# Seven block products for the first 1024 rows of the first layer's output projection

## The chip, the cores and the metric

The kernel runs on one core of a Trainium2 chip. The metric is the device time of one execution in microseconds (us). Before the change three runs gave 829.10, 829.45 and 830.46 us, a median of 829.45 us.

## The reference, cut to what matters

Four residual layers on an input of 256 positions by 1024 channels, all in float32. Layers 0 and 3 are the gated MLP below, layer 1 is an attention layer, layer 2 a pooling layer.

```python
def mixer_a(h, w_in, v_gain, w_s, b_s, w_out):
    proj = h @ w_in                                   # (256, 1024) @ (1024, 6144)
    u, v, z = proj[..., :2048], rms_norm(proj[..., 2048:4096], v_gain), proj[..., 4096:]
    ...                                               # mixed: lower-triangular ws over 128 positions, plus b_s
    y = u * mixed * jax.nn.silu(z)
    return y @ w_out                                  # (256, 2048) @ (2048, 1024)

def reference(x, norm_gain, a_w_in, ...):
    for i in range(4):
        h = rms_norm(x, norm_gain[i])
        y = mixer(i)(h, ...)                          # A, B, C, A
        x = x + y
    return x
```

The change concerns `y @ w_out` of layer 0, and of that the first 1024 of the 2048 rows of `w_out`.

## The kernel before

**One product.** TensorE (PE) multiplies in a rounded 32-bit format. Each float32 operand is kept as a high part (rounded) and a low part (the rest), and one product is three matmuls: high by high (L87), high by low (L88), low by high (L89), in `mm3`. A matmul has 128 rows of the contraction, 128 positions and at most 512 columns.

**The weight stream.** All weights come in one sequence of units of 512 KB (128 partitions, two contraction blocks, 512 columns). SyncE (SP) issues a load into one of four raw buffers (`wr`; `load_units`, L177), ScalarE (ACT) writes the high part `w..h` (L92), VectorE (DVE) the low part `w..l` (L95). Seven pairs of high and low parts exist. A raw buffer is free for the next load when the low part of its unit is done, so the load of unit i follows the low part of unit i − 4. In layer 3 two more raw buffers take part. Units are split up to five ahead of the matmuls that use them.

**The order of work.** Each engine does its instructions in the order in which the program writes them. The program writes in steps: each step emits the matmuls of half a unit, lets the tasks that are due emit theirs (`tick`), and then emits splits for coming units. A task that gives a number waits for so many ticks. So a DVE instruction emitted by a task stands behind all splits that were emitted before it.

**Accumulators.** Four PSUM banks (`pp`, one 128x512 float32 result each) take the projections, three take attention and mixing, and one takes transposes (`yp`). A bank is given to the next user when the reader of its last content is done.

**Layer 0.** Units 0 to 15 are v, 16 to 47 alternate z and u in four groups of 512 columns, 48 to 63 are `w_out` ("wo"), 64 is the first of layer 1. Group n of y is made by `y_task`: two DVE multiplications by u (L664), four by the mixed values (L669, shown as pairs), four transposes on PE for each half of the positions (`yp`, L677), a high part on ACT and a low part on DVE (`y0nh`, `y0nl`). Group 3, the last, is made while wo already runs. `proj_out` takes 16 contraction blocks against two column halves: a unit holds two blocks and one column half and is used for both halves of the positions, 12 matmuls of 128x512. Four accumulators `wo` stay open through it; the last four blocks are done position half by position half, and DVE adds each accumulator into the residual `x` (L546).

**Block products that exist already.** In layer 3 three of the z/u groups are done as seven products of half-sized blocks in place of eight (`seven_products`). They need sums of the quarters of the weights, which `sums_of_quarters` makes long before: it loads a quarter of a part's columns into a buffer (`stage`, or `qs`, which shares the buffer `xs`), makes four additions on DVE (L194), and stores the sums to DRAM (`sums`); `PARTS` says how many such parts are made beside layers 0, 1 and 2. They also need sums of quarters of h (12 DVE passes of 128x512 with four high parts on ACT).

Of the kernel before, what the change touches and what calls it, by code (L numbers as in the profile page):

```python
# [17 lines left out]
P = 128  # L18
# [28 lines left out]
SEVEN = (0, 2, 3)  # L47
PARTS = (4, 8, 8)
# [3 lines left out]
def hybrid_trunk_kernel(ctx, tc, x, wts, norm_gainT, a_v_gain, a_wsT, a_bsT, b_gl, b_gv, c_scaleT,  # L52
# [92 lines left out]
    sums = {(n, j): dp.tile([4, P, UNIT], F32, name=f"sums{n}{j}") for n in SEVEN for j in range(2)}  # L145

    def seven_units(n):

        return n_units - 48 + 8 * n + (8 if n == 3 else 0)

    for n in reversed(SEVEN):
        z = seven_units(n)
        seq[z:z + 8] = [e[j] for e in (((n, 0, 0), (n, 0, 1)), (z, z + 1), (z + 6, z + 7), ((n, 3, 0), (n, 3, 1)),
                                       (z + 2, z + 3), ((n, 2, 0), (n, 2, 1)), ((n, 1, 0), (n, 1, 1)))
                        for j in range(2)]
    n_seq = len(seq)

    raw_users = {"wr": [-1] * RAW_BUFS, "xs": [-1], "wx": [-1]}

    def raw_place(i):  # L160

        return ("wr", "wr", "wr", "wr", "xs", "wx")[i % 6] if i >= n_units - 48 else "wr"
# [18 lines left out]
    def sums_of_quarters(parts, shared=False, delay=0, wait=2):  # L181
# [5 lines left out]
        for n, j, c in parts:  # L187
            z = seven_units(n) + j
            cs = slice(c * 256, (c + 1) * 256)
            q = cp.tile([P, 4, 256], F32, tag="xs", name=f"qs{n}{j}{c}", bufs=1) if shared else stage  # L190
            nc.sync.dma_start(q, wts[z:z + 8:2][:, :, cs].rearrange("i p c -> p i c"))
            yield 7
            for a, b in ((0, 2), (2, 3), (3, 0), (1, 3)):
                nc.vector.tensor_tensor(q[:, a], q[:, a], q[:, b], op=ALU.add)  # L194
                yield 1
            yield wait
            nc.sync.dma_start(sums[n, j][:, :, cs].rearrange("i p c -> p i c"), q)
            yield 4
# [318 lines left out]
    def proj_out(layer, nkt, yT, k0=0):  # L517


        acc = [[[(slice(0, HALF), pp(f"wo{layer}_{t}{n}"))] for n in range(2)] for t in range(2)]  # L520
# [4 lines left out]
        for j in range(k0 // 2, jt):  # L525
            for n in range(2):
                w = next_unit()
                for kk in range(2):
                    k = 2 * j + kk
                    for t in range(2):  # L530
                        for cs, o in acc[t][n]:
# [6 lines left out]
        for t in range(2):  # L538
            for i, (j, n, w) in enumerate(tail):
# [26 lines left out]
                tick()  # L566

# [15 lines left out]
    def layer_a(layer, consts, pl, mid):  # L583
# [101 lines left out]

        if layer == DEPTH - 1:
            smh, sml = pair(pl, [P, 4, 4, P], "sm", f"sm{layer}", 1)

        def sums_task():
            q = {}  # L690
            for k, t in ((1, 1), (0, 1), (0, 0), (1, 0)):
                d = q[k, t] = tmp("sz", f"sq{layer}{k}{t}", 4).rearrange("p (k c) -> p k c", c=P)
# [669 lines left out]
```

## Time and profile before

| | |
|---|---|
| median of three runs | 829.45 us |
| the profiled execution's own time | 829.75 us |
| its span | 828.0 us |
| PE busy | 821.5 us |
| DVE busy | 612.7 us |
| ACT busy | 515.0 us |
| first matmul of wo in layer 0 | 147.67 us |
| first matmul of layer 1 (`qk`) | 193.05 us |

The span is the time from the first to the last instruction that the profiler saw; 1.75 us of the profiled execution lie around it. In a timeline row the first number is the start in microseconds, the second the time that the row took, then come the engine, the line, the operation, output <- inputs by the program's names, the shape, and how many instructions the row joins; in square brackets, how long the engine had been idle and who released it. The start of a matmul counted from the start of the one before is what PE needs for one; the durations of neighbours overlap. The same holds for DVE, where a row's duration is a little longer than the distance to the next.

### The profile page before, as it was taken

How to read it: one execution, taken by the hardware profiler on the slowest of the kernel's cores; microseconds unless marked ns; L12 is line 12 of the kernel's file. 1: busy time of each engine (PE TensorE's matmuls, PEld its weight loads, DVE VectorE, ACT ScalarE, POOL GpSimd, SP SyncE). 2: the span in 40 equal slices, each digit the busy share in tenths (PEclk: the TensorE clock that was granted, in tenths of full speed). 3: DMA queues.
4: the chain of work that ended last, by engine and by line, in shares of the span. 5: the costliest groups of instructions: out<-in, count | busy, mean ns of one | idle time of the engine just before them, and what ended most of it. 6: DMA issues, size and time to landing. Idle time of an engine off the chain costs nothing.

```text
span 828.0 us, 12649 instructions
## 1 busy us (share of the span) xinstructions
PE 821.5 (99%) x4585; PEld 711.2 (86%) x4585; DVE 612.7 (74%) x1054; ACT 515.0 (62%) x947; POOL 46.3 (6%) x69
## 2 busy tenths in 40 slices
PE   9999999999999999999999999999999999999998
PEld 7888888888988888888888889999988888788887
DVE  5887656646768678678678577798874799979683
ACT  7775444436768687687688567436643668656570
POOL 1201000000000010010010012000000000000000
PEclk9999999999999999999999999999999999999999
DMA  8878666662888668577567268647786378868661
GB/s 280 289 270 274 225 224 192 219 200 79 296 269 255 200 201 275 184 225 257 190 199 222 78 200 286 224 159 236 227 284 220 102 249 276 284 206 323 204 261 51
DMA packets 70111, 184.21 MB, mean 222 GB/s; under 512 B 5952, under 2 KB 31312, under 8 KB 69920
## 3 DMA queue, kind: packets, MB, share of 16 engines
q1 hardware_dynamic: 68784, 179.33, 65.1%
q0 software_dynamic: 976, 3.79, 1.4%
q8 instruction: 36, 0.59, 0.3%
q10 hardware_dynamic: 288, 0.28, 0.2%
q14 instruction: 27, 0.22, 0.1%
HBM read 169.74 MB, written 13.63 MB: 221 GB/s over the span
## 4 chain that ended last, share of the span: by engine, by line
PE 98%; DMA 1%; DVE 0%; issue 0%; POOL 0%; ACT 0%; ACTq 0%
PE qk L89 5%; PE qk L87 5%; PE qk L88 5%; PE wo L87 5%; PE wo L88 5%; PE wo L89 5%; PE v L88 5%; PE v L87 5%; PE v L89 5%; PE z L89 2%; PE z L87 2%; PE u L87 2%; PE u L88 2%; PE z L88 2%; PE u L89 2%; PE cz L89 2%
## 5 line engine op out<-in xcount | busy, mean ns | idle before, releaser
L849 POOL TENSOR_TENSOR qr<-qm,m 128x8 f32<-128x8 f32 x12 | 20.1, 1674 | 228.1 <-DVE qm L848 228.1
L844 ACT ACTIVATE junk<-qk 128x128 bf16<-128x128 f32 x96 | 26.6, 277 | 5.6 <-PE qk L89 3.0
L853 ACT ACTIVATE qn<-qk,qr 128x128 f32<-128x128 f32 x96 | 27.5, 381 | 3.7 <-POOL qr L849 3.7
L194 DVE TENSOR_TENSOR stage<-stage 128x256 f32<-128x256 f32 x64 | 26.9, 421 | 2.6 <-DMA stage<-in_wts_dram 2.1
L320 ACT ACTIVATE hT<-hp,gT 128x128 fp32r<-128x128 f32 x48 | 13.0, 384 | 14.9 <-PE hp L316 14.9
L546 DVE TENSOR_TENSOR x<-wo,x 128x512 f32<-128x512 f32 (+1 forms) x16 | 10.8, 674 | 13.3 <-PE wo L89 13.3
L302 POOL TENSOR_TENSOR r<-ms,m 128x1 f32<-128x1 f32 x6 | 4.2, 708 | 273.9 <-DVE ms L299 273.9
L325 DVE SCALAR_TENSOR_TENSOR hT<-hp,gT,hT 128x128 fp32r<-128x128 f32 x48 | 13.5, 344 | 7.4 <-ACT hT L320 7.4
L844 ACT ACTIVATION_READ_ACCUMULATOR junk<-qk 128x1 f32 x96 | 18.9, 197 | 0.0
L294 ACT ACTIVATE junk<-x 128x512 bf16<-128x512 f32 x16 | 10.2, 639 | 10.1 <-DVE x L546 9.9
L194 DVE TENSOR_TENSOR qs<-qs 128x256 f32<-128x256 f32 x32 | 13.4, 419 | 3.6 <-DMA qs<-in_wts_dram 3.5
L848 DVE TENSOR_SCALAR qm<-qs 128x8 f32<-128x8 f32 x12 | 2.1, 172 | 18.4 <-ACT junk L844 18.4
L943 ACT ACTIVATE p<-p,rl 128x384 f32<-128x384 f32 (+1 forms) x16 | 11.5, 769 | 6.1 <-DVE rl L942 6.1
L664 DVE SCALAR_TENSOR_TENSOR sz<-u,m,sz 128x512 f32<-128x512 f32 x8 | 6.0, 746 | 11.7 <-PE u L89 11.7
L874 PE MATMUL qt<-ident,qn 128*128 128x128 f32 x96 | 14.5, 274 | 0.1
L874 PEld LDWEIGHTS qt<-ident,qn 128*128 128x128 f32 x96 | 11.3, 140 | 3.2 <-issue 1.4
L866 DVE TENSOR_TENSOR rb<-qn,kcb 128x32 f32<-128x32 f32 x96 | 13.8, 186 | 0.0
L602 DVE TENSOR_TENSOR vv<-v,kc 128x512 f32<-128x512 f32 x16 | 10.7, 686 | 3.4 <-ACT junk L600 3.1
L939 ACT ACTIVATE p<-p,nb 128x768 f32<-128x768 f32 x8 | 7.5, 938 | 7.3 <-DVE nb L938 7.3
L862 DVE TENSOR_TENSOR ra<-qn,kcb 128x64 f32<-128x64 f32 x48 | 10.6, 221 | 0.8 <-ACT qn L853 0.2
L974 PE MATMUL pt<-ident,p 128*128 128x128 f32 x48 | 9.9, 275 | 0.0
L797 ACT ACTIVATE sz<-z,m 128x512 f32<-128x512 f32 x8 | 5.4, 688 | 6.9 <-PE z L89 6.9
(2963 smaller groups left out, 3349.1 us busy)
## 6 DMA issues: line engine op xcount, KB each, us to landing
wr<-in_wts_dram SPq DMA_DIRECT2D x258, 512.0 KB, 4.4
wr<-sums SPq DMA_DIRECT2D x20, 512.0 KB, 4.6
stage<-in_wts_dram SPq DMA_DIRECT2D x16, 512.0 KB, 5.1
sums<-stage SPq DMA_DIRECT2D x16, 512.0 KB, 6.2
qs<-in_wts_dram SPq DMA_DIRECT2D x8, 512.0 KB, 5.3
sums<-qs SPq DMA_DIRECT2D x8, 512.0 KB, 5.0
wx<-in_wts_dram SPq DMA_DIRECT2D x7, 512.0 KB, 5.4
wx<-sums SPq DMA_DIRECT2D x4, 512.0 KB, 4.5
```

The lines of the kernel that those rows point to most:

```text
L87: nc.tensor.matmul(out_ap, lh[0], rh[0], start=start, stop=False, skip_group_check=True)
L88: nc.tensor.matmul(out_ap, lh[0], rh[1], start=False, stop=False, skip_group_check=True)
L89: nc.tensor.matmul(out_ap, lh[1], rh[0], start=False, stop=stop, skip_group_check=True)
L194: nc.vector.tensor_tensor(q[:, a], q[:, a], q[:, b], op=ALU.add)
L320: nc.scalar.activation(h_parts(layer)[0][:, k, t * P:(t + 1) * P], pt[:, k % 4], AF.Copy, scale=gT[:, layer, k:k + 1])
L325: nc.vector.scalar_tensor_tensor(hTl, pt[:, k % 4], gT[:, layer, k:k + 1], hTh.bitcast(F32), op0=ALU.mult, op1=ALU.subtract)
L844: nc.scalar.activation(junk[:, :HD], ov[t][:, h], AF.Square, accum_out=ssq[t][:, h:h + 1])
L849: nc.gpsimd.tensor_tensor(rqs, ms, m05_row[:, :8], op=ALU.pow)
L853: nc.scalar.activation(qn[t][:, h], ov[t][:, h], AF.Copy, scale=rq[t][:, h:h + 1])
L866: nc.vector.tensor_tensor(rb[:, hs, s0:s0 + 16], qn[t][:, hs, s1:s1 + 16], c, op=ALU.mult)
L874: nc.tensor.transpose(pts[t][:, h], qn[t][:, h], ident)
L943: nc.scalar.activation(f, f, AF.Copy, scale=rl[i][:, 0:1])
```

## The change

The first 1024 rows of `w_out` (units 48 to 55 before: eight units of 12 matmuls of 128x512, 96 in all) are taken as a two by two block product of four blocks of y (position half by 512 rows) with four blocks of weights (512 rows by 512 columns), and done as seven products of 12 matmuls, 84 in all. Each product takes two units, and a unit is used for 6 matmuls. Eight of the fourteen units hold sums of the weight quarters and are loaded from DRAM (`sums`); the stream has 14 units there in place of 8. The other half of `w_out` follows as before, 8 units (62 to 69), and layer 1 begins with unit 70.

- The products go into four banks: `xw` (used for three products, the second and third being added on the first), `yw`, `zw` (two) and `ww`. After each product DVE adds or subtracts the bank's content into `x`, eight additions in all. `proj_out` takes its four banks when it first uses them.
- Sums of blocks of y are made by `y_sums` from `left_sums`, as in layer 3: 12 DVE passes and four high parts on ACT, while z and u of the last groups run. It uses `wx` and one new tile.
- Sums of weight quarters: beside layer 0 there were 4 parts, now there are 12, in two chains that begin after the first v projection; one works in `stage` on 8 parts, the other in `xs` on 4. `PARTS` goes from (4, 8, 8) to (8, 4, 8, 8). A part is 0.5 MB in, four additions, 0.5 MB out. The longer chain runs on through wo.
- `sums_task` of layer 3 becomes a call of the common `left_sums`; its order of work stays.

```diff
-SEVEN = (0, 2, 3)
-PARTS = (4, 8, 8)
+BLOCKS = {("wo", 0): 48, ("zu", 0): -48, ("zu", 2): -32, ("zu", 3): -16}
+PARTS = (8, 4, 8, 8)
...
-        acc = [[[(slice(0, HALF), pp(f"wo{layer}_{t}{n}"))] for n in range(2)] for t in range(2)]
+        acc = [[[], []], [[], []]]
+
+        def bank(t, n):
+            if not acc[t][n]:
+                acc[t][n].append((slice(0, HALF), pp(f"wo{layer}_{t}{n}")))
...
+    def part_product(o, a, first):
+        for j in range(2):
+            w = next_unit()
+            for kk in range(2):
+                k = 2 * j + kk
+                mm3(o, a(k), (w[0][:, kk], w[1][:, kk]), first and k == 0, k == 3)
+                step(kk, due=kk == 1)
...
+    def proj_seven(layer, yT, smh, sml):
+        def add(t, n, o, op=ALU.add):
+            xh = xt[t][:, n * HALF:(n + 1) * HALF]
+            nc.vector.tensor_tensor(xh, xh, o, op=op)
+            yield 1
+
+        def quarter(k, t):
+            return lambda i: yT(4 * k + i, t)
+
+        xb = pp(f"xw{layer}")
+        part_product(xb, quarter(0, 0), True)
+        spawn(add(0, 0, xb), 1)
+        yb = pp(f"yw{layer}")
+        part_product(yb, quarter(1, 0), True)
+        spawn(add(0, 0, yb), 1)
+        need(("sums", layer))
+        zb = pp(f"zw{layer}")
+        part_product(zb, sum_tile(smh, sml, S_A21_A22), True)
+        spawn(add(1, 1, zb), 1)
+        part_product(xb, sum_tile(smh, sml, S_REST), False)
+        spawn(add(0, 1, xb, ALU.subtract), 1)
+        part_product(zb, sum_tile(smh, sml, S_A12_REST), False)
+        spawn(add(0, 1, zb), 1)
+        part_product(xb, sum_tile(smh, sml, S_A11_A21), False)
+        spawn(add(1, 1, xb, ALU.subtract), 1)
+        spawn(add(1, 0, xb), 1)
+        wb = pp(f"ww{layer}")
+        part_product(wb, quarter(1, 1), True)
+        spawn(add(1, 0, wb), 1)
...
+            if layer == 0 and n == 0:
+                spawn(sums_of_quarters(parts[:4] + parts[8:8 + PARTS[1]], False, 8, 1, 6))
+                spawn(sums_of_quarters(parts[4:8], True, 15, 1, 6))
...
-        if layer == 0:
-            spawn(sums_of_quarters(parts[:PARTS[0]]))
+        def y_sums():
+            while ("y", layer, 1) not in done:
+                yield 1
+            room = [wx[:, 0], wx[:, 1], tmp("yq", "yq", 1)]
...
+            yield from left_sums(layer, y_quarter, place, smh, sml, ("sums", layer), 2)
+
         for n in range(4):
+            if n == 2 and ("wo", layer) in BLOCKS:
+                spawn(y_sums(), 4)
...
-        proj_out(layer, 16, get, KT if layer == DEPTH - 1 else 0)
+        if ("wo", layer) in BLOCKS:
+            proj_seven(layer, get, smh, sml)
+        proj_out(layer, 16, get, KT if layer == DEPTH - 1 or ("wo", layer) in BLOCKS else 0)
```

What this makes of the order on DVE, around the start of wo. Before, the rows from the last group's multiplications on (`sz` and `yy` are the two multiplications, `w53l` the low part of unit 53, `y03l` the low part of y's last group, one row for each half of the positions):

```order
L664 SCALAR_TENSOR_TENSOR sz_1264<-u_0_1268,m_77,sz_1264 128x512
L669 SCALAR_TENSOR_TENSOR yy_1363<-mx_1306,bs_267,sz_1264 128x256 x2
L664 SCALAR_TENSOR_TENSOR sz_1266<-u_1_1269,m_77,sz_1266 128x512
L669 SCALAR_TENSOR_TENSOR yy_1367<-mx_1313,bs_267,sz_1266 128x256 x2
L95 TENSOR_TENSOR w53l<-wr_1287,w53h 128x1024
L95 TENSOR_TENSOR y03l<-yp_1390,y03h 128x4x128
L95 TENSOR_TENSOR w54l<-wr_1321,w54h 128x1024
L95 TENSOR_TENSOR y03l<-yp_1415,y03h 128x4x128
L95 TENSOR_TENSOR w55l<-wr_1340,w55h 128x1024
L95 TENSOR_TENSOR w56l<-wr_1359,w56h 128x1024
L95 TENSOR_TENSOR w57l<-wr_1397,w57h 128x1024
```

After it only low parts of units stood there. Now, behind the same four rows of multiplications (in the changed file L97 is the low part, L198 the addition of weight quarters, L636 the addition into x):

```order
L198 TENSOR_TENSOR stage<-stage 128x256
L97 TENSOR_TENSOR w53l<-wr_1345,w53h 128x1024
L198 TENSOR_TENSOR stage<-stage 128x256
L97 TENSOR_TENSOR w54l<-wr_1379,w54h 128x1024
L198 TENSOR_TENSOR stage<-stage 128x256
L97 TENSOR_TENSOR y03l<-yp_1451,y03h 128x4x128
L636 TENSOR_TENSOR x<-x,xw_1427 128x512
L97 TENSOR_TENSOR w55l<-wr_1397,w55h 128x1024
L198 TENSOR_TENSOR stage<-stage 128x256
L97 TENSOR_TENSOR w56l<-wr_1415,w56h 128x1024
L97 TENSOR_TENSOR y03l<-yp_1486,y03h 128x4x128
L636 TENSOR_TENSOR x<-x,yw_1460 128x512
```

Four additions of quarters and the first additions into x have come in between, and `y03l` has moved from behind one low part to behind two. Further on DVE, rows that follow at once:

```order
L97 TENSOR_TENSOR w57l<-wr_1439,w57h 128x1024
L97 TENSOR_TENSOR w58l<-wr_1458,w58h 128x1024
L636 TENSOR_TENSOR x<-x,zw_1495 128x512
L97 TENSOR_TENSOR w59l<-wr_1474,w59h 128x1024
L97 TENSOR_TENSOR w60l<-wr_1493,w60h 128x1024
L636 TENSOR_TENSOR x<-x,xw_1427 128x512
L97 TENSOR_TENSOR w61l<-wr_1508,w61h 128x1024
L97 TENSOR_TENSOR w62l<-wr_1521,w62h 128x1024
L636 TENSOR_TENSOR x<-x,zw_1495 128x512
L97 TENSOR_TENSOR w63l<-wr_1534,w63h 128x1024
L97 TENSOR_TENSOR w64l<-wr_1546,w64h 128x1024
L636 TENSOR_TENSOR x<-x,xw_1427 128x512 x2
```

Two low parts stand ahead of each addition; behind these rows come `w65l`, `w66l` and the addition of `ww`. On PE, at the second unit of the second half of `w_out` (`wo_00` to `wo_11` are its four accumulators, by position half and column half; L89, L90 and L91 are the three matmuls of a product in the changed file):

```order
L91 MATMUL wo_10_1630<-w62h,y02l 128x512
L89 MATMUL wo_01_1648<-w63h,y02h 128x512 [waits DVE_49,Activation_49]
L90 MATMUL wo_01_1648<-w63l,y02h 128x512
L91 MATMUL wo_01_1648<-w63h,y02l 128x512
L89 MATMUL wo_11_1652<-w63h,y02h 128x512 [waits DVE_49]
```

The first matmul of `wo_01` and of `wo_11` waits for the addition that empties the bank it takes over, those of `xw` and `ww`; one unit earlier `wo_10` waits in the same way for that of `zw`. Before, the four accumulators of wo were open from its start, and nothing in wo waited for an addition. On SP, the same stretch of the changed program's queue (`sums` are the stored sums):

```order
L181 DMA wr_1493<-sumswo_69 128x1024
L181 DMA wr_1508<-sumswo_70 128x1024
L201 DMA sumszu_71<-stage 128x4x256
L181 DMA wr_1521<-in_wts_dram 128x1024
L181 DMA wr_1534<-in_wts_dram 128x1024
L181 DMA wr_1546<-in_wts_dram 128x1024
L181 DMA wr_1559<-in_wts_dram 128x1024
L195 DMA stage<-in_wts_dram 128x4x256
L181 DMA wr_1572<-in_wts_dram 128x1024
```

A store of 0.5 MB of sums now goes ahead of the load of unit 62 (`wr_1521`), and a load of a part ahead of that of unit 66 (`wr_1572`). Before, no transfer of the chain stood in this stretch of the queue.

More of the change, by code (lines that the diff above doesn't have):

```diff
@@ L517, in proj_out @@
     def proj_out(layer, nkt, yT, k0=0):
-        acc = [[[(slice(0, HALF), pp(f"wo{layer}_{t}{n}"))] for n in range(2)] for t in range(2)]
+        acc = [[[], []], [[], []]]
+        def bank(t, n):
+            if not acc[t][n]:
+                acc[t][n].append((slice(0, HALF), pp(f"wo{layer}_{t}{n}")))
+        if ("wo", layer) not in BLOCKS:
+            for t in range(2):
+                for n in range(2):
+                    bank(t, n)
         if layer == DEPTH - 1:
@@ L566, in proj_out, with left_sums, full, parted @@
                 tick()
+    S_A21_A22, S_A11_A21, S_REST, S_A12_REST = range(4)
+    def left_sums(name, quarter, place, smh, sml, key, pause=1):
+        def full(k, t):
+            d = place(f"sq{name}{k}{t}").rearrange("p (k c) -> p k c", c=P)
+            hh, hl = (a.bitcast(F32) for a in quarter(k, t))
+            nc.vector.tensor_tensor(d, hh, hl, op=ALU.add)
+            return d
+        def parted(i, d):
+            hi_of(smh[:, i], d)
+            yield pause
+            lo_of(sml[:, i], d, smh[:, i])
+            yield pause
+        a22 = full(1, 1)
+        yield pause
+        a21 = full(0, 1)
+        yield pause
+        nc.vector.tensor_tensor(a22, a21, a22, op=ALU.subtract)
+        yield from parted(S_A21_A22, a22)
+        a11 = full(0, 0)
+        yield pause
+        nc.vector.tensor_tensor(a21, a11, a21, op=ALU.subtract)
+        yield from parted(S_A11_A21, a21)
+        nc.vector.tensor_tensor(a11, a22, a11, op=ALU.subtract)
+        yield from parted(S_REST, a11)
+        a12 = full(1, 0)
+        yield pause
+        nc.vector.tensor_tensor(a12, a12, a11, op=ALU.add)
+        yield from parted(S_A12_REST, a12)
+        done.add(key)
@@ L712, in sm @@
             def sm(i):
-                return lambda k: (smh[:, i, k], sml[:, i, k])
-            def product(o, a, first):
-                for j in range(2):
-                    w = next_unit()
-                    for kk in range(2):
-                        k = 2 * j + kk
-                        mm3(o, a(k), (w[0][:, kk], w[1][:, kk]), first and k == 0, k == 3)
-                        step(kk, due=kk == 1)
+                return sum_tile(smh, sml, i)
+            product = part_product
             def minus(o, name):
@@ L1045, in layer_b @@
                 if hp == 0 and g == 0:
-                    n1, n2 = sum(PARTS[:2]), sum(PARTS)
-                    spawn(sums_of_quarters(parts[PARTS[0]:n1]))
+                    n0, n1, n2 = (sum(PARTS[:i]) for i in (2, 3, 4))
+                    spawn(sums_of_quarters(parts[n0:n1]))
                     spawn(sums_of_quarters(parts[n1:n2], True, 9))
@@ L1205, in hybrid_trunk_kernel @@
     box = {}
-    parts = [(n, j, c) for n in SEVEN for j in range(2) for c in range(4)]
+    parts = [(b, j, c) for b in BLOCKS for j in range(2) for c in range(4)]
     def after_ws():
```

71 lines of the change are left out of this document (34 added, 37 removed).

## The prediction

> **What bounds the kernel now.** I read the busy shares, the granted clock and the chain that ended last, then PE's waits, then the windows of the stretches that the change touches, then the timelines there.
>
> ```profile
> PE 821.5 (99%) x4585; PEld 711.2 (86%) x4585; DVE 612.7 (74%) x1054; ACT 515.0 (62%) x947; POOL 46.3 (6%) x69
> PEclk9999999999999999999999999999999999999999
> PE 98%; DMA 1%; DVE 0%; issue 0%; POOL 0%; ACT 0%; ACTq 0%
> PE warm L286 <- DVE wx L65: 1.1, 1, 1.1
> PE xb L87 <- ACT n L725: 0.7, 1, 0.7
> ```
>
> PE is busy 821.5 of 828.0 us at full clock and makes 98% of the last chain. Its longest wait inside the layers is 0.7 us, in layer 3's seven products. So a matmul taken away is worth its time, if PE meets no new wait.
>
> ```profile
> 47.00:147.00 100.00, 100.00 (x477) 83.68 (x476) 67.55 (x90) 49.70 (x58) 4.25 (x8) 1.00 0.71 233
> 147.00:176.00 29.00, 29.00 (x133) 24.03 (x132) 17.76 (x19) 11.47 (x12) 0.00 (x0) 1.00 0.62 206
> 697.00:717.00 20.00, 19.35 (x91) 15.90 (x91) 19.84 (x21) 15.23 (x19) 1.44 (x2) 1.00 0.88 309
> ```
>
> The columns are length, PE, weight loads, DVE, ACT, POOL, clock, DMA share, GB/s. DVE, at 74% overall, is busy 17.76 of 29 us where wo begins (147 to 176), and 19.84 of 20 in a seven-product stretch of layer 3 (697 to 717). The question is what happens when the first becomes like the second.
>
> **What is saved.** A unit of wo:
>
> ```profile
> 147.67 0.39 PE L87 MATMUL wo<-w48h,y00h 128*128 128x512 f32 x1
> 159.52 0.39 PE L87 MATMUL wo<-w52h,y01h 128*128 128x512 f32 x1
> 162.24 0.39 PE L87 MATMUL wo<-w53h,y01h 128*128 128x512 f32 x1
> ```
>
> Unit 52 to 53 is 2.72 us for 12 matmuls, 0.2267 each. 96 become 84: **−2.72 us**. From 48 to 52 there are 11.85 us, four units and two sets of transposes, so a set costs (11.85 − 10.88)/2 = 0.485.
>
> The Trainium skill ("TensorE: Matmul & The Clock Gate", section "Wait — 56ns, not 53.3ns?") gives 215.7 ns from one matmul of 512 columns to the next; by that the saving would be 2.59 us. The trace's 226.7 ns does not agree, and decides.
>
> **What it adds to DVE before wo.** By the order, 20 more additions of quarters, plus 12 passes for the sums of y, fall before the last group's multiplications. Prices:
>
> ```profile
> 63.16 0.88 DVE L194 TENSOR_TENSOR stage<-stage 128x256 f32<-128x256 f32 x2
> 63.95 1.22 DVE L95 TENSOR_TENSOR w24l<-wr,w24h 128x1024 fp32r<-128x1024 f32 x1
> 65.09 0.88 DVE L194 TENSOR_TENSOR stage<-stage 128x256 f32<-128x256 f32 x2
> 708.28 0.69 DVE L753 TENSOR_TENSOR p<-yb,p 128x512 f32<-128x512 f32 x1
> 708.88 1.22 DVE L95 TENSOR_TENSOR w239l<-wx,w239h 128x1024 fp32r<-128x1024 f32 x1
> ```
>
> From start to start an addition of quarters takes 0.79/2 = 0.395, a low part 1.14, a pass of 128x512 0.60. That is 20 x 0.395 + 12 x 0.60 = 15.1 us in the 100 us from 47 to 147, where DVE is busy 67.55. It fits, also with twice the transfers:
>
> ```profile
> 198.00:248.00 50.00, 50.00 (x321) 45.13 (x320) 34.80 (x74) 35.48 (x84) 3.40 (x2) 1.00 0.77 253
> 73.42 1.23 DVE L95 TENSOR_TENSOR w28l<-wr,w28h 128x1024 fp32r<-128x1024 f32 x1 [3.83 <-ACT w28h L92]
> 86.96 0.39 PE L87 MATMUL u<-w28h,hT 128*128 128x512 f32 x1
> ```
>
> From 198 to 248 two such chains run and PE loses nothing. Unit 28, the one whose split came latest for its load, was ready at 74.65 and first used at 86.96: 12.3 us of cover. I cost this part at nothing; if loads came more than 12 us late it would cost the excess.
>
> **What it adds to DVE in the seven products.** A unit now lasts 6 x 0.2267 = 1.36 us on PE; its low part takes 1.14 on DVE, so little is left for eight additions into x, four of quarters and two low parts of y. Ahead of them stand the last multiplications of y:
>
> ```profile
> 147.19 0.75 DVE L664 SCALAR_TENSOR_TENSOR sz<-u,m,sz 128x512 f32<-128x512 f32 x1 [3.91 <-PE u L89]
> 147.98 0.88 DVE L669 SCALAR_TENSOR_TENSOR yy<-mx,bs,sz 128x256 f32<-128x256 f32 x2
> 148.77 0.74 DVE L664 SCALAR_TENSOR_TENSOR sz<-u,m,sz 128x512 f32<-128x512 f32 x1
> 149.55 0.88 DVE L669 SCALAR_TENSOR_TENSOR yy<-mx,bs,sz 128x256 f32<-128x256 f32 x2
> 150.34 1.22 DVE L95 TENSOR_TENSOR w53l<-wr,w53h 128x1024 fp32r<-128x1024 f32 x1
> ```
>
> They wait for u (3.91 us idle), so DVE enters at 147.19 as before and comes out at 150.34.
>
> ```profile
> 154.88 0.69 DVE L95 TENSOR_TENSOR y03l<-yp,y03h 128x512 fp32r<-128x512 f32 x1 [1.04 <-ACT y03h L92]
> ```
>
> A `y03l` takes 0.69 until what waits for it may start, and 0.60 until the next row, like the other passes of 128x512. From 150.34 I add up the new order at the prices above, in the clock of before; PE starts the first product at 147.67, and each product takes 2.72.
>
> 1. *Transposes.* Three additions, two low parts and `y03l` end at 150.34 + 3 x 0.395 + 2 x 1.14 + 0.69 = 154.50. The second set of `yp` needs the only transpose bank, which this `y03l` reads. PE has done two products and a set at 147.67 + 5.44 + 0.485 = 153.60: **stall 0.90**. Then set and third product to 157.70, fourth to 160.42.
> 2. *Fifth product (`zw` again).* It waits for the addition of `zw`, which stands behind w57l and w58l. From 154.41 on: four low parts, one addition of quarters, one `y03l`, two additions into x, then that of `zw`: 154.41 + 4.56 + 0.395 + 3 x 0.60 + 0.69 = 161.85. **Stall 1.43.** Done 164.57.
> 3. *Sixth (`xw` again).* Two low parts and an addition later, 164.73: stall 0.16, if the low parts need not wait for loads.
> 4. *Second half of wo.* `wo_11` takes the bank of `ww`, whose addition stands behind w65l and w66l. From 164.64 on: six low parts (w61l to w66l), three additions, then that of `ww`: 164.64 + 6.84 + 1.80 + 0.69 = 173.97. PE, with stall 0.16, comes there at 164.73 + 2 x 2.72 + 2.72 + 0.68 = 173.57: **stall 0.40**.
>
> Sum without load waits: 0.90 + 1.43 + 0.16 + 0.40 = 2.89 against 2.72 saved, **+0.17**.
>
> **Loads.** A load follows the low part four units before, then lands, then gets its high part:
>
> ```profile
> 157.00 1.07 ACT L92 ACTIVATE w57h<-wr 128x1024 fp32r<-128x1024 f32 x1 [0.26 <-PE wo L89]
> DMA to landing us min/median/max: 3.1/4.4/9.8
> wr<-in_wts_dram SPq DMA_DIRECT2D x258, 512.0 KB, 4.4
> stage<-in_wts_dram SPq DMA_DIRECT2D x16, 512.0 KB, 5.1
> sums<-stage SPq DMA_DIRECT2D x16, 512.0 KB, 6.2
> ```
>
> The lap of a raw buffer is landing + 1.07 + 1.22, 6.7 us at the median 4.4 (4.4 to landing, min 3.1, max 9.8). Four units at PE's new pace last only 4 x 1.36 = 5.44. So loads begin to bind. Two places:
> - w56l ends about 157.8; w60l can start at 157.8 + 4.4 + 1.07 = 163.3 in place of 162.90, which makes the sixth product's stall 0.16 + 0.40 = **0.56**.
> - w58l ends at 161.2. Then come two laps, units 62 and 66, and the addition of `ww` (0.69): 161.2 + 2 x 2.29 + 0.69 + both landings = 166.5 + both. Unit 62 goes behind a store of sums and 66 behind a load of a part, so I take 4.4 for one and 5.1, as beside the chain's own traffic, for the other: 176.0. PE comes at 173.97 now: **stall 2.0** in place of 0.40. With 3.1 twice it is 172.7, and DVE alone decides; with 6.2 twice, as stores take, 178.9 and a stall of 4.9.
>
> Sum: 0.90 + 1.43 + 0.56 + 2.0 = 4.9 of stalls, less 2.72: **+2.2**. Afterwards a unit again lasts 2.72 on PE, and splitting catches up within some units.
>
> **The boundary to layer 1.** Eight additions of quarters stand in wo's tail and among the next layer's norm:
>
> ```profile
> 196.12 0.88 DVE L310 TENSOR_SCALAR xs<-x,r 128x512 f32<-128x512 f32 x2
> 197.18 1.04 PE L316 MATMUL hp<-ident,xs 128*128 128x128 f32 x8
> ```
>
> PE transposes `xs` right after DVE made it; one addition of quarters (0.395) stands ahead of it now. Nothing to 0.4; I take 0.2.
>
> Together +2.4 on the profiled execution's own 829.75: 832.15. That execution is 0.3 above the median of the runs, so against it **831.8 us**.
>
> **Rivals.**
> - *A, fully covered.* −2.72: 826.7. For it: in layer 3's seven products DVE is as full (19.84 of 20) and PE loses 0.65. Against: there ACT copies the accumulators out at once,
>
> ```profile
> 704.73 0.57 ACT L725 ACTIVATE n<-xb 128x512 f32<-128x512 f32 x1
> 705.36 0.50 PE L87 MATMUL xb<-w234h,sm3h 128*128 128x512 f32 x1 [0.65 <-ACT n L725]
> ```
>
>   and even so PE waits 0.65 for that 0.57 us copy. Two more raw buffers serve there as well. Here additions stand behind two low parts each. It decides if DVE comes 2.9 us earlier through the queue than my sum. 8%.
> - *B, loads never bind* (landings near 3.1): +0.17 to +0.4, 829.6 to 829.9 against the median. 24%.
> - *C, landings of 6.2 in the seven products*: stalls 0.90 + 1.43 + 0.56 + 4.9 − 2.72 + 0.2 = +5.3: 834.7. For it: a store and a part's load share the queue; against: DMA is busy 0.62 here. 10%.
> - *D, the clock falls after a stall.* The only window of the trace with PE idle for long,
>
> ```profile
> 815.00:828.00 13.00, 9.65 (x54) 8.27 (x53) 2.93 (x5) 0.00 (x0) 0.00 (x0) 0.96 0.22 81
> ```
>
>   shows a clock of 0.96 at PE busy 9.65 of 13. My longest stall is 2.0 us. If a product then ran at half pace it would add 2.72: 834.5. 2%. The Trainium skill, "TensorE: Matmul & The Clock Gate", section "A second HAM failure mode: psum-queue depth-cycling", tells of a kernel that cycled through PSUM banks, where short idles between groups made the clock swing between half and full; its section "What's actually happening" has an idle window of about 3.4 us for that. The traced row with the 0.65 us stall shows full clock in its window (1.00), so no run here shows it.
> - *It doesn't do what it says*: the order shows 84 matmuls in the place of 96, so I give it nothing.
>
> **How the numbers follow.** The forecast (830.5 to 833.5) has 56%, A 8%, B 24%, C 10%, D 2%. The range of 8 in 10 leaves out A and the far end of C and D; it takes in B, with 0.8 below for a stall of 0.90 that might not come, and C: 828.8 to 834.7. A measurement of this kernel tells about 0.2% from no change, that is 827.8 to 831.1. Faster is A, 8%. Same is B and the low end of the forecast, 24 + 4 = 28%. Slower is the rest, 64%.
>
> **What would show it.** PE's waits should name the low part of y before the second `yp` (0.9), and the additions into x before the second use of `zw` (1.4), the second and third of `xw` (0.6), and `wo_11` (2.0). DVE should be near full from 147 to 176, ACT should wait for `wr` loads near units 62 and 66, and PE should wait nowhere in v, z and u. The next layer began here:
>
> ```profile
> 193.05 0.39 PE L87 MATMUL qk<-w64h,hT 128*128 128x512 f32 x1
> ```
>
> From the first matmul of the first product to the first `qk` the time before was 193.05 − 147.67 = 45.4; I expect 47.8. If no wait at `wo_11` shows, the load term is wrong and B holds; if waits stand before 147, the cover is.

## The result, and the profile after

The changed kernel takes 839.9 us in the median of four runs (839.0 to 841.1), beside 829.6 for the kernel before: a ratio of 1.0124, 95% interval 1.0107 to 1.0142. It is slower by 10.3 us; the forecast was slower by 2.4, at 831.8 with an upper end of 834.7. The profiled execution took 840.14 us, its span is 838.4.

The page of the changed kernel: busy shares, granted clock in 40 slices, and the chain that ended last.

```profile
PE 823.8 (98%) x4573; PEld 710.1 (85%) x4573; DVE 640.8 (76%) x1112; ACT 523.4 (62%) x957; POOL 43.8 (5%) x69
PEclk9999999989999999999999999999999999999999
PE 80%; DVE 8%; DMA 6%; ACT 3%; issue 3%; POOL 0%; ACTq 0%; DVEq 0%
```

PE has 12 instructions fewer and is busy 2.3 us longer: some of them ran slower. One slice of the clock, the ninth (168 to 189 us), is below 9. The chain, 98% PE before, now runs through DVE and DMA as well. What PE waits for in the changed kernel (total, times, longest):

```profile
PE wo L89 <- DVE x L636: 3.7, 2, 2.6
PE zw L89 <- DVE x L636: 1.2, 1, 1.2
PE xb L89 <- ACT n L797: 1.1, 1, 1.1
PE yp L772 <- DVE yy L764: 1.0, 1, 1.0
PE yp L772 <- DVE y03l L97: 0.6, 1, 0.6
PE xw L89 <- DVE x L636: 0.4, 1, 0.4
```

L636 is the addition into x, L764 the multiplication of y by the mixed values, L797 a copy by ACT in layer 3. Following the first use of each unit through both traces places the loss: the products begin at 149.52 (147.67 before), layer 1 at 201.90 (193.05 before). Of the 10.4 us between the spans, 1.85 are lost up to the products, 7.0 from there to layer 1, 0.5 early in layer 1, 0.9 in layer 3; the rest is the rounding of these.

**The waits in the products, on PE.** The timeline of the changed kernel, where the second half of wo begins; `w63` serves `wo_01` first, then `wo_11`:

```profile
175.04 0.39 PE L91 MATMUL wo<-w62h,y02l 128*128 128x512 f32 x1
176.53 0.47 PE L89 MATMUL wo<-w63h,y02h 128*128 128x512 f32 x1 [1.10 <-DVE x L636]
176.84 0.40 PE L90 MATMUL wo<-w63l,y02h 128*128 128x512 f32 x1
177.07 0.40 PE L91 MATMUL wo<-w63h,y02l 128*128 128x512 f32 x1
180.03 0.79 PE L89 MATMUL wo<-w63h,y02h 128*128 128x512 f32 x1 [2.56 <-DVE x L636]
180.62 0.63 PE L90 MATMUL wo<-w63l,y02h 128*128 128x512 f32 x1
...
184.89 0.58 PE L91 MATMUL wo<-w64h,y02l 128*128 128x512 f32 x1
185.31 0.40 PE L89 MATMUL wo<-w64h,y02h 128*128 128x512 f32 x1
```

A wait of 1.10, three matmuls, a wait of 2.56, and then twelve matmuls from 180.03 to 185.31, 5.28 us where 2.72 is usual. Two things are to be read here. The bracket counts from the modelled end of the last matmul, 0.39 after its start, though the next could have followed after 0.23, and the first after a wait takes 0.31: a wait costs its bracket plus 0.16 until PE goes on, and about 0.08 more for its slow start. And the clock fell (columns as before; the seventh after the engines is the granted clock):

```profile
172.00:176.00 4.00, 3.43 (x15) 2.46 (x14) 4.00 (x6) 2.65 (x3) 0.00 (x0) 1.00 1.01 345
176.00:180.00 4.00, 0.94 (x3) 0.48 (x3) 3.37 (x5) 2.15 (x3) 0.00 (x0) 0.81 0.95 342
180.00:184.00 4.00, 3.97 (x9) 3.13 (x10) 3.97 (x7) 2.08 (x2) 0.00 (x0) 0.50 0.85 267
184.00:188.00 4.00, 4.00 (x16) 3.20 (x15) 2.07 (x2) 1.46 (x2) 0.00 (x0) 0.84 0.89 223
```

**The same place on DVE and ACT.** DVE's rows ahead of those two waits, in order:

```profile
168.45 1.23 DVE L97 TENSOR_TENSOR w61l<-wr,w61h 128x1024 fp32r<-128x1024 f32 x1 [1.65 <-ACT w61h L94]
171.10 1.22 DVE L97 TENSOR_TENSOR w62l<-wr,w62h 128x1024 fp32r<-128x1024 f32 x1 [1.42 <-ACT w62h L94]
172.25 0.68 DVE L636 TENSOR_TENSOR x<-x,zw 128x512 f32<-128x512 f32 x1
172.84 1.22 DVE L97 TENSOR_TENSOR w63l<-wr,w63h 128x1024 fp32r<-128x1024 f32 x1
173.98 1.22 DVE L97 TENSOR_TENSOR w64l<-wr,w64h 128x1024 fp32r<-128x1024 f32 x1
175.11 1.27 DVE L636 TENSOR_TENSOR x<-x,xw 128x512 f32<-128x512 f32 x2
176.31 1.22 DVE L97 TENSOR_TENSOR w65l<-wr,w65h 128x1024 fp32r<-128x1024 f32 x1
178.16 1.23 DVE L97 TENSOR_TENSOR w66l<-wr,w66h 128x1024 fp32r<-128x1024 f32 x1 [0.63 <-ACT w66h L94]
179.30 0.68 DVE L636 TENSOR_TENSOR x<-x,ww 128x512 f32<-128x512 f32 x1
```

The addition of `ww` could have run when its product ended, at 172.5; it ran at 179.30, because `w65l` and `w66l` stood ahead, units that PE needs only at 187 and 190. These wait for ACT, and ACT for their loads; the first row is SP's, the load of unit 62, which took the buffer that `w58l` had freed at 162.8:

```profile
162.84 0.33 SPq L181 DMA_DIRECT2D wr<-in_wts_dram  x1
167.36 1.06 ACT L94 ACTIVATE w61h<-wr 128x1024 fp32r<-128x1024 f32 x1 [2.41 <-DMA wr<-sumswo]
170.01 1.06 ACT L94 ACTIVATE w62h<-wr 128x1024 fp32r<-128x1024 f32 x1 [1.59 <-PE xw L91]
177.07 1.06 ACT L94 ACTIVATE w66h<-wr 128x1024 fp32r<-128x1024 f32 x1 [1.55 <-DMA wr<-in_wts_dram]
DMA to landing us min/median/max: 4.6/5.9/7.1
```

The last line is for the loads that were issued from 160.5 to 173, units 61 to 66. Unit 62 took the longest, 7.1 us, and landed at 169.9, just before ACT began on it. (The bracket there names PE, but PE had done with the pair of buffers that `w62h` writes, that of unit 55, since 162.3.) Unit 66 took 4.6 us.

**In z and u**, the first group's multiplications of y on DVE, and the transposes that need them on PE; the first two rows are the same instructions before the change:

```profile
75.42 0.88 DVE L669 SCALAR_TENSOR_TENSOR yy<-mx,bs,sz 128x256 f32<-128x256 f32 x2
77.84 0.60 PE L677 MATMUL yp<-ident,yy 128*128 128x128 f32 x4
76.15 1.23 DVE L97 TENSOR_TENSOR w28l<-wr,w28h 128x1024 fp32r<-128x1024 f32 x1 [2.27 <-ACT w28h L94]
77.30 0.74 DVE L759 SCALAR_TENSOR_TENSOR sz<-u,m,sz 128x512 f32<-128x512 f32 x1
78.08 0.88 DVE L764 SCALAR_TENSOR_TENSOR yy<-mx,bs,sz 128x256 f32<-128x256 f32 x2
78.71 0.74 PE L772 MATMUL yp<-ident,yy 128*128 128x128 f32 x4 [1.02 <-DVE yy L764]
```

Unit 28 itself is needed only at 88.3. What PE missed were the multiplications of y, queued on DVE behind its low part. Before, they were done at 76.3 and needed at 77.84, 1.5 us of cover. Now `w28l` began 2.73 us later (76.15 for 73.42), which leaves 1.2 us: the bracket of 1.02 and the 0.16.

### The profile page after: what moved, and what is told of

It is laid out like the page before. It is cut to its first block, busy times and chain, and to the rows that moved or that the text cites. A ratio compares the mean times of both kernels' runs of the same rounds, so it can differ in the third digit from the quotient of the medians.

```text
span 838.4 us, 12737 instructions
## 1 busy us (share of the span) xinstructions
PE 823.8 (98%) x4573; PEld 710.1 (85%) x4573; DVE 640.8 (76%) x1112; ACT 523.4 (62%) x957; POOL 43.8 (5%) x69
## 4 chain that ended last, share of the span: by engine, by line
PE 80%; DVE 8%; DMA 6%; ACT 3%; issue 3%; POOL 0%; ACTq 0%; DVEq 0%
PE qk L91 5%; PE qk L89 5%; PE qk L90 5%; DMA wr<-in_wts_dram 5%; PE wo L89 4%; PE wo L91 4%; PE wo L90 4%; PE v L89 2%; PE v L91 2%; PE v L90 2%; PE cz L91 2%; PE cz L89 2%; PE cz L90 2%; PE cx L89 2%; PE cx L90 2%
## 5 line engine op out<-in xcount | busy, mean ns | idle before, releaser
L198 DVE TENSOR_TENSOR stage<-stage 128x256 f32<-128x256 f32 x80 | 33.5, 419 | 2.4 <-DMA stage<-in_wts_dram 1.9
L198 DVE TENSOR_TENSOR qszu<-qszu 128x256 f32<-128x256 f32 x32 | 13.4, 420 | 0.4 <-DMA qszu<-in_wts_dram 0.2
L772 PEld LDWEIGHTS yp<-ident,yy 128*128 128x128 f32 x64 | 7.5, 139 | 5.3 <-issue 1.4
L772 PE MATMUL yp<-ident,yy 128*128 128x128 f32 x64 | 9.9, 277 | 2.0 <-DVE yy L764 1.0
L697 DVE TENSOR_TENSOR vv<-v,kc 128x512 f32<-128x512 f32 x16 | 10.3, 682 | 0.7 <-ACT junk L695 0.7
```

Source lines behind the costliest of these rows:

```text
L198: nc.vector.tensor_tensor(q[:, a], q[:, a], q[:, d], op=ALU.add)
L772: nc.tensor.transpose(pt[:, k], ys[t][:, k * P:(k + 1) * P], ident)
```

## The experiments

In the table, "products" is the time from the first matmul of wo's first half to the first `qk`, from each profile.

| kernel | median us | ratio to before (95%) | products us |
|---|---|---|---|
| before | 829.6 | | 45.38 |
| the change | 839.9 | 1.0107 to 1.0142 | 52.38 |
| e2 six raw buffers | 836.63 | 1.0072 to 1.0102 | 47.62 |
| e4 filler in the waits | 838.87 | 1.0098 to 1.0132 | 49.12 |
| e5 chain moved to layer 2 | 836.57 | 1.0063 to 1.0106 | 46.60 |
| e6 additions earlier | 834.56 | 1.0048 to 1.0078 | 46.99 |
| e7 = e2 and e6 | 834.05 | 1.0037 to 1.0067 | 45.60 |
| e8 = e5, e7, layer 3's buffers | 832.38 | 1.0029 to 1.0061 | 43.91 |
| e9 = e7, chain moved to layer 1 | 829.65 | 0.9997 to 1.0015 | 44.03 |
| e18 = e9, constants moved | 829.04 | 0.9987 to 1.0005 | 44.73 |

### The transfers of the chain, and the number of raw buffers

First try, moving four parts of the chain to layer 1:

```diff
-PARTS = (8, 4, 8, 8)
+PARTS = (8, 0, 12, 8)
```

> The second half of the longer chain of sums (four parts, begun at the end of z and u and run on through wo) is made beside layer 1 instead; all else as in the change. Theory T1 (the chain's store and load beside the fourteen units make the landings of units 61 to 66 long, and its four additions delay DVE): the landings fall from 5.6-7.1 us to about 4.5, the waits of PE before the second half of wo (1.10 and 2.56 us in the changed kernel) fall under 0.5 together, the clock stays at 1.00 there, the waits at the second yp and at zw fall by about 0.6 each; from first matmul of the products to first qk about 46 in place of 52.4 us, and the time is about 833 to 834. Rival R1 (four raw buffers alone make the laps long): waits of over 3 us before the second half of wo remain, and the time stays above 838.

That chain had not ended when layer 2's began, and both work in `stage`: in the trace two parts are loaded into it, at 498.79 and 505.97 us, with no store between them. So layer 3's sums were mixed, and the run (849.58 us) tells nothing. The same idea with the four parts in layer 2 (e5):

```diff
-PARTS = (8, 4, 8, 8)
+PARTS = (8, 0, 8, 8)
...
-        spawn(sums_of_quarters(parts[sum(PARTS):], wait=8))
+        spawn(sums_of_quarters(parts[sum(PARTS):], wait=2))
```

> The four parts that ran on through wo are made beside layer 2 instead (eight parts there, with shorter pauses); raw buffers and order of the additions into x as in the change. Theory T2 (the waits in the products have two sources: DVE's queue, and landings stretched by the DMA rate): without the four additions of quarters the wait of the second yp goes (0.59 to 0), that at zw falls from 1.22 to about 0.2; without 1 MB of the chain's transfers the landings of units 61 to 66 fall from 5.6-7.1 us to about 5, the waits before the second half of wo from 3.66 to 1.5 or less, and the clock stays near 1.00. From the first matmul of the products to the first qk 46 to 47 us in place of 52.4; time 833 to 834.5. Rival R1 (the lap over four raw buffers is long by itself): the waits before the second half stay above 3 us, time above 837.

The products took 46.6 us, inside the expectation, and the landings in that stretch 3.8/4.5/5.2 us (min, median, max) in place of 4.6/5.9/7.1. The wait at the second `yp` was gone; 0.69 at zw, 0.93 at the second use of `xw` and one wait of 1.46 us at the second half of wo were left. R1 falls: with the same four raw buffers and without the chain's transfers the laps are shorter. The total, 836.57, is above what was expected, since layer 3 now waited 1.7 us where the longer chain ran on beside it, and z and u lost 1.7 in that profile.

With the traffic left and two more raw buffers (e2):

```diff
     def raw_place(i):
+        if 56 <= i < 70:
+            return ("wr", "wr", "wr", "wr", "xs", "wx")[(i - 56) % 6]
```

> Two more raw buffers (xs and wx, free by then) take part in the ring for units 56 to 69; the order on DVE and the chain stay as in the change. Theory T1 (traffic): the same 1 MB of the chain stays, but it can be moved earlier, since the DMA engines were busy only 0.45 from 150 to 160; if lap and traffic act together, the landings stay long but start two units earlier, the waits before the second half of wo fall from 3.66 to about 0.4 us (what DVE alone gives), the clock stays at 1.00, time about 834. Rival R2 (the DMA rate itself binds, a unit of 0.5 MB each 1.36 us being over the 345 GB/s seen): waits there stay above 2 us and the time above 837.

Between the two: 47.62 us. One wait of 2.16 us remains, at `wo_11`, against two of 3.66 together; T1 had 0.4 there, R2 over 2, though the time, 836.63, stays just under R2's 837. Its DMA share and GB/s (last two columns) against time:

```profile
150.00:160.00 10.00, 9.41 (x46) 7.52 (x45) 9.96 (x17) 5.58 (x7) 0.00 (x0) 1.00 0.42 147
160.00:172.00 12.00, 10.78 (x48) 8.37 (x47) 10.68 (x12) 6.45 (x7) 0.00 (x0) 1.00 1.01 356
172.00:176.00 4.00, 3.31 (x15) 2.42 (x13) 3.54 (x5) 2.33 (x3) 0.00 (x0) 1.00 1.05 396
```

In the change the same three stretches have 146, 299 and 345 GB/s. So two more raw buffers do bring in more, 356 and 396, but the DMA share is then 1.01 and 1.05 from 160 on, and each load takes longer (6.1/8.8/9.3 us there). From 150 to 160 the share stood at 0.42: with DVE busy 9.96 of 10 us, low parts came late and raw buffers were not freed.

### The order on DVE

e6 emits each addition right behind its product's last matmul, so that one low part stands ahead of it and not two:

```diff
...
                 mm3(o, a(k), (w[0][:, kk], w[1][:, kk]), first and k == 0, k == 3)
+                if k == 3:
+                    for e in last:
+                        spawn(e)
                 step(kk, due=kk == 1)
...
```

> Only the order on DVE changes: the addition that empties a bank is emitted right behind the product's last matmul, so one low part ahead of it instead of two. Theory T2: zw 1.22 to about 0.1 us, xw 0.42 to about 0, wo_11 about 1.1 less; the second yp waits up to 0.6 more, since an addition stands ahead of y03l now; the clock dip shrinks with the idle time. Time 836 to 837.5. Rival R5 (loads alone decide): the waits at zw and xw go, but those before the second half grow by the same amount, time 839 to 840.

It did more than expected: 834.56, products 46.99. The waits at zw and xw were gone, that at the second `yp` rose from 0.6 to 1.2, and one of 1.8 was left at wo. So the position of eight additions, with the same work and the same transfers, is worth over 5 us of the 10; about half of that is the slow clock, 2.56 us in the change, which did not come here (mean clock 0.999 to 1.000 in its four runs). R5 falls. With six raw buffers as well (e7):

> Six raw buffers (as tried before: 836.6 us, one wait of 2.16 us left at wo_11, where the addition of ww stands behind the low parts of units 65 and 66, which landed 8.8 us after issue) and the additions one low part earlier. Theory T2: the wait at wo_11 falls by about 1.2 us to 1.0 or less, that at zw from 1.2 to 0.1; time 834 to 835. Rival R2 (the DMA rate alone): the wait at wo_11 stays near 2 us, time 836 or more.

The wait at `wo_11` fell from 2.16 to 1.2, the time to 834.05, products 45.60. Then all edits, and the extra raw buffers of layer 3 three units earlier, as before the change (e8):

> Six raw buffers, the additions one low part earlier, the chain's four parts moved to layer 2, and in layer 3 the two extra raw buffers three units earlier, as they stood before the change. Theory T2: all waits in the products under 0.5 us together; from the first matmul of the products to the first qk 43 to 44 us against 45.4 before the change; layer 3's wait for ACT falls from 1.1 back to 0.7; left are the losses in z and u (up to 2 us). Time 828 to 831. Rival R2 (a unit each 1.36 us asks for 385 GB/s, more than the DMA engines gave): about 2 us of waits remain in the products, time 832 or more.

The products take 43.91 us, 1.47 less than the eight before: of the 2.72 promised, half is left; most of the rest goes into waits of 0.3 and 0.2 and their restarts. But 3.3 us were lost again in layers 2 and 3, where the longer chain now ran (a wait of 1.7 at layer 3's first products), so the total is 832.38, above the expected 831. Layer 3's buffers did not settle anything: its wait for ACT was 0.9 with them, and 0.4 in e7 without. With the four parts spread over both chains of layer 1 (`PARTS = (8, 0, 10, 10)`, shorter pauses) and layer 3 as in the change (e9):

> Six raw buffers and the additions one low part earlier, as in the run of all edits, but the four moved parts are made beside layer 1 (two more in each of its chains, with shorter pauses), and layer 2 keeps its four parts; the raw buffers of layer 3 as in the change. Theory T3 (the products themselves now save what the matmuls promise; in the run of all edits, first use of layer 1 was 1.26 us earlier than before the change, and 3.3 us were lost again where the longer chain ran in layers 2 and 3): layers 2 and 3 lose under 1 us, z and u 0 to 1.5, time 828 to 830. Rival R6 (a chain of that size costs PE its 2 to 3 us wherever it stands): new waits in layer 1, time 831 to 833.

829.65 us, level with before; layers 1 and 2 lost nothing, so R6 falls. In its profile the products gained 1.35, z and u lost 1.93 and layer 3 lost 1.3. That execution took 831.43 us, near the upper end of its eleven runs (828.75 to 832.12), so the typical run loses less than it shows.

### The clock

e4 gives PE filler where it waits at `wo_01` and `wo_11`:

```diff
...
+                        if layer == 0 and k == k0 and n == 1:
+                            fill = ident.bitcast(BF16)
+                            for _ in range(10 if t == 0 else 24):
+                                nc.tensor.matmul(warm[:, :2 * P], fill[:, :P], fill[:, :2 * P], start=True, stop=True,
+                                                 skip_group_check=True)
...
```

> As the change, but PE does 10 and 24 filler matmuls of 128x256 (results unused) where it waits before the first matmul of wo_01 and of wo_11. Theory T1: the clock of 0.5 from 180 to 185 follows the idle time of PE between 175 and 180; with the filler the clock stays at 1.00, the eleven matmuls that took 0.427 us take 0.227 again, and the time falls by about 2.2 us to 837.7. Rival R4 (the low clock is not due to the idle time, or filler does not count): the clock dips as before and the time stays at 839.9 or rises.

```profile
174.35 1.27 PE L549 MATMUL warm_wo<-ident 128*128 128x256 bf16 x10
175.59 0.47 PE L89 MATMUL wo<-w63h,y02h 128*128 128x512 f32 x1
...
176.36 2.79 PE L549 MATMUL warm_wo<-ident 128*128 128x256 bf16 x24
178.91 0.47 PE L89 MATMUL wo<-w63h,y02h 128*128 128x512 f32 x1
179.23 0.39 PE L90 MATMUL wo<-w63l,y02h 128*128 128x512 f32 x1
```

`wo_11` begins 7.3 us after the end of the seventh product (171.6 to 178.9), in the change 7.5 (172.5 to 180.0), so the waits are as long; but the matmuls behind it follow at 0.23 us: the dip is gone, and R4 falls. Products 49.12, 3.3 less than in the change, of which 2.56 are the dip. The timed runs show less, 838.87 against 839.9, where 2.2 less was expected: the price of 2.56 is read from the trace of the change, and the times bear out only part of it. From run to run a lower clock mostly goes with a longer time: e8's four runs at a mean clock of 1.000 took 831.9 to 832.5 us, its two at 0.998 took 833.9 and 836.5; e2's two at 1.000 took 835.5 and 836.2, its two at 0.997 took 837.0 and 838.3. e5 does not fit: 836.2 at 1.000, but 834.3 at 0.998.

### What the sums cost in z and u

All sums made, but wo with plain units (e3), and the same with only the eight parts of wo in layer 0 (e12). The main step of the edit:

```diff
...
-        if ("wo", layer) in BLOCKS:
-            proj_seven(layer, get, smh, sml)
-        proj_out(layer, 16, get, KT if layer == DEPTH - 1 or ("wo", layer) in BLOCKS else 0)
+        proj_out(layer, 16, get, KT if layer == DEPTH - 1 else 0)
...
```

> All sums of the change are made (twelve parts of weight quarters in two chains, the sums of y), but wo is done as before, with eight plain units and 96 matmuls; the sums for wo are not read. Theory T1: the losses outside wo belong to the sums alone: about +2.1 us in z and u (the wait of yp on yy at 78.7 and its neighbours), 0.5 at the boundary, and up to 0.9 in layer 3: 831.7 to 833.2. Rival R3 (these come from the seven products or are chance): no wait in z and u, 829 to 830.5.

> The sums of the change in z and u only (eight parts for wo, the sums of y; the other parts beside layers 1 and 2), wo done as before with plain units, the sums for wo not read. All theories: 1 to 2.5 us over the kernel before, 830.5 to 832.

e3 took 832.51 (1.0024 to 1.0051), e12 831.55 (1.0015 to 1.0032): the sums alone cost 2 to 3 us without any product. Not all of it lies in z and u: in the two profiles wo begins at 148.54 and 148.59, 0.9 us late, and of the 2.2 and 2.0 us by which the spans are longer most of the rest is lost in layer 3 (a wait of 1.56 and 1.58 for ACT's copy, 0.65 before). Then e10 (on e9) and e11 (on the change) moved the last low part behind the multiplications of y:

```diff
-                step(kk)
+                step(kk, AHEAD - 1 if name in ("u00", "u01", "u02") and k == KT - 1 else AHEAD)
```

> As the run before, and in layer 0 the low part of the unit that is split last at the end of a group's u is emitted behind the group's multiplications of y, not ahead of them. Theory T3 (the losses in z and u come from the multiplications of y standing on DVE behind a low part whose load is late): the wait of yp on yy near 78 is gone in every profile, and the time is 0.3 to 1 us under that of the run before. Rival R7 (PE waits there for DVE's amount of work, not for its order): the same waits, the same time.

> The change with only that edit: in layer 0 the group's multiplications of y stand ahead of the last low part. Theory T3: the wait of yp on yy near 78.7 (1.02 us) goes, first use of wo is about 1 us earlier against before the change (+0.9 in place of +1.85), the products are as in the change; time about 839. Rival R7: the wait stays, or moves to the low part of y.

The wait near 78 went and others came: 0.8 at the low part of y02 in e10; 0.5 and 1.5 at y00 and y02 in e11. The times, 831.74 (829.65 without the edit) and 840.72 (839.9 without it), are no better. So this order alone is not it, as R7 had it. Taking the parts' additions out, or their transfers (e13 and e14, both on e12 and only for the eight parts of wo, whose sums are not read):

> As the run before, but the eight parts of layer 0 are only loaded and stored, without their 32 additions on DVE. Theory T4 (transfers make the loads late, and DVE waits for them with the multiplications of y behind): the same 1 to 2 us over before, waits of PE on yy or y02l near 78 or 130 remain. Rival R8 (DVE's amount of work): the waits go, the time is within 0.5 us of before.

> As the first of these runs, but the eight parts are neither loaded nor stored, only the 32 additions are made, on one buffer that holds zeros. Theory T4: the wait near 78 goes, the landings of units 25 to 33 are near 4.5 us, time within 0.7 us of before. Rival R8: time as in the first of these runs.

830.31 (1.0003 to 1.0020) with transfers alone, 830.16 (1.0000 to 1.0017) with additions alone, 831.55 with both. Neither T4 nor R8 is right: over the whole kernel transfers alone cost 0.9 us, additions alone 0.7, both 2.1. In z and u the profiles show nothing for either alone (wo begins at 147.72 and 147.63, with no wait near 78), and 0.9 for both. Starting the second chain about 5 us later on e9 (e15, delay 19 in place of 15):

> The version that came out level with the kernel before (829.65 us), with the second chain of layer 0 starting four ticks, about 5 us, later. Theory T4: the wait near 78 depends on which transfers meet the loads of units 27 to 29, so it moves or shrinks; time 828.5 to 830. Rival R8: no change, 829.65 within its spread.

837.74 (1.0086 to 1.0113): worse by 8 us. In the profiles wo begins 5.35 us later than in e9, most of it from one place. DVE, PE and two windows of it:

```profile
79.14 0.42 DVE L200 TENSOR_TENSOR qswo<-qswo 128x256 f32<-128x256 f32 x1 [6.73 <-DMA qswo<-in_wts_dram]
82.03 1.09 PE L769 MATMUL yp<-ident,yy 128*128 128x128 f32 x4 [4.41 <-DVE yy L761]
70.00:80.00 10.00, 7.61 (x34) 5.97 (x32) 3.27 (x5) 1.84 (x2) 0.00 (x0) 1.00 0.99 342
80.00:90.00 10.00, 7.97 (x29) 6.53 (x30) 9.44 (x18) 4.27 (x6) 0.00 (x0) 0.66 0.63 216
```

An addition of the chain stood on DVE ahead of the multiplications of y, and waited 6.73 us for its part, which took 10 us to land; then PE idled 4.41 us and the clock fell to 0.66. The trace gives a suspect: near 67 us POOL sends layer 1's constants, about 0.8 MB, just as the chains store and load. e16 and e17 moved their place in the program 30 ticks on:

```diff
-        spawn(load_b())
+        spawn(load_b(), 30)
```

> The version that came out level (829.65 us: six raw buffers, additions one low part earlier, moved parts beside layer 1), and layer 1's constants loaded 30 ticks (about 41 us) later, near 107 in place of 66. Theory T5 (the cost of the sums in z and u is that their transfers meet these constants and make the loads of units 26 to 29 land after 8 to 10 us): landings there about 6 us, no wait of yp on yy near 78, first use of layer 1 1 to 1.5 us earlier than before the change, time 828 to 829. Rival R9 (any of the chains' transfers do it): the wait near 78 stays at 0.5 to 1.5 us, time 829.2 to 830.

> The kernel with the sums alone and plain wo (831.55 us), with the constants later in the same way. Theory T5: 830 to 830.6, no wait near 78. Rival R9: 831 to 832.

830.49 (1.0005 to 1.0022) and 831.11 (1.0017 to 1.0036), and in e16's trace the constants left from 66.9 to 68.0 us, in e9's from 66.1 to 67.2: POOL has nothing to wait for ahead of them, so a later place in its program is no later time. They tell nothing of T5; e16 is in effect e9 once more, 0.8 us slower. With the four constants issued by SP (e18, `nc.sync.dma_start` for `nc.gpsimd.dma_start`, on e9):

> As the run with the constants later, which did not move them: POOL had nothing ahead of them, so they left at 66.9 us as before. Now SP issues them, in its order behind the loads of units up to 38, near 107 us. Theory T5: without them the loads of units 27 to 29 land in about 6 us in place of 8.6 to 8.9, the wait of yp on yy near 79 goes, first use of layer 1 is 1 to 1.5 us earlier than before the change, time 828 to 829. Rival R9 (any of the chains' transfers do it): the wait stays at 0.5 to 1.5 us, time 829.5 to 830.5.

The loads issued from 67 to 72 land in 5.6/6.0/6.7 us (in e9, from 67 to 71, in 8.3/9.6/9.9), and PE waits nowhere in z and u. The stretch from 60 to 80 and the beginning of the products of e18:

```profile
60.00:80.00 20.00, 20.00 (x97) 16.78 (x96) 16.89 (x24) 13.26 (x14) 1.22 (x3) 1.00 0.85 301
150.00:172.00 22.00, 21.63 (x98) 17.00 (x96) 20.48 (x23) 14.40 (x15) 0.00 (x0) 1.00 0.83 292
```

829.04 us, against 829.21 for the kernel before on the same chip. None of its eleven runs is above 829.51, while four of e9's eleven are above 830.5. That speaks for T5 but does not show it: e8 has the same program as e9 up to the products, its constants too are sent by POOL (from 64.3 to 65.5, in e9 from 66.1 to 67.2), and its profile has no wait in z and u either (its products begin at 147.88). e18 also changes the engine that issues the constants, and not only their time. Layer 1 begins 0.74 us earlier than before the change, not the expected 1 to 1.5, since a wait of 0.93 came at `wo_11`; layer 3 gives about as much back (a wait of 1.23 for ACT's copy). The best version is level with the kernel before (0.9987 to 1.0005), no more.

## Why the prediction was wrong

The direction was right, and most of the loss lies where the forecast put it; the size was not right. The forecast counted a stall from when PE could have gone on, so for the stalls in the products 0.16 us is added to each bracket below. By its own steps:

- **Saved 2.72.** Right as far as the runs show: e8 and e9 have products 1.47 and 1.35 us shorter than the eight, with a few waits left.
- **Stalls 1 to 3.** Right: 0.75, 1.38 and 0.58, against 0.90, 1.43 and 0.56. DVE's queue added up from single prices gave each stall to within 0.15 us.
- **Second half of wo, 2.0.** Mis-sized: 1.26 at `wo_01` and 2.73 at `wo_11`, 4.0 together. The path was the one forecast, from `w58l` over the landings of units 62 and 66 to the addition of `ww`. What failed was the landings, put at 4.4 and 5.1, medians over the whole kernel: they took 7.1 and 4.6, together 11.7 where the forecast had 9.5 and rival C (10%) had 12.4. Fourteen units in the time of seven, with a store and a load of the chain, fill the DMA engines (a share of 1.01 from 172 to 176), and the traced share of 0.62 that was held against rival C belonged to a stretch that asked for half as many units. e5 shows the chain's part in it, e2 the rate's.
- **The first matmul after a wait.** The forecast had no term for it: it takes 0.08 us longer, 0.4 us for the five waits.
- **Rival D, 2%.** This is the step that failed most: the sum put a slow clock at nothing, and the clock fell, for 2.56 us where the rival had 2.72. It was weighed as an alternative to the forecast, by the longest single stall, and it was an addition to it, set off by two waits with three matmuls between. e4 shows the cause; the price is that of the trace. That the rival's price came near it is chance, since nothing in its working said how long the clock would stay low.
- **Sums in z and u at nothing.** Wrong: 1.85 up to the products, and waits before 147 are what the forecast had named as the sign that the cover is wrong. The cover was read from when PE needs unit 28 (86.96); the multiplications of y behind its low part on DVE were needed at 77.84, 9.1 us earlier, and had 1.5 us of cover, not 12.3. The profiles of e12 to e14 show 0.9 us in z and u from transfers and additions together and nothing from either alone. Whether layer 1's constants set it off stays open: e18 without them there shows no wait, but neither does e8 with them.
- **Boundary 0.2.** Nothing was lost there. Not foreseen was 0.5 in layer 1's first head (a wait of 0.4 at `qt`).
- **Not foreseen:** 0.9 us in layer 3, where the wait for ACT's copy rose from 0.65 to 1.07 and a new one of 0.28 came. The first varied from 0.3 to 1.6 in the experiments, with the raw buffers as before or not; its cause stays open.

Together: −2.72 + 2.71 of stalls 1 to 3 + 3.99 + 0.4 + 2.56 is 6.9 of the 7.0 us measured in the products.

The Trainium skill, "TensorE: Matmul & The Clock Gate", section "What's actually happening", has the clock halve after an idle window of about 3.4 us. The clock of 0.50 agrees. By that figure the window was not idle throughout, for the longest wait was 2.56 us, and three matmuls stood between it and the wait of 1.10. How much work in the window still counts as idle no run here shows; e2's single wait of 2.16 us left the clock at 1.00 in its profiled run.

## What to carry to other kernels

An instruction that frees something PE waits for must not stand, in an in-order queue, behind work whose inputs come by DMA and are needed later: here eight additions moved by one place were worth over 5 us, about half of it the slow clock that did not come. Cover is to be read for everything behind the late instruction on its engine, not for that instruction's own result. And when PE is at 99%, the price of adding waits is not their sum: two gaps of 1.10 and 2.56 us close together also cost a slow clock behind them here, so a term for the clock belongs into the forecast as soon as the stalls of one place add up to about as much.

## What was not expected of the hardware

- Waits of 1.10 and 2.56 us within 4.6 us (175.4 to 180.0) halved the clock for some 5 us; a single one of 2.16 us did not in the profiled run of e2, while two of its four runs had a mean clock of 0.997, at a place that is not known.
- Two more raw buffers brought in more, but each load took longer: with six the loads took 6.1 to 9.3 us at 356 and 396 GB/s, with four 4.6 to 7.1 us at 299 and 345 GB/s (160 to 172 and 172 to 176).
- A transfer that POOL issues left when POOL reached it: 30 ticks later in the program the constants left from 66.9 us, beside 66.1.
